# The order of a two-block network's steps on one Trainium2 core: found by a dry run, or written out as a table

## The chip, the core and the metric

The kernel runs on one core of a Trainium2 chip. The metric is the device time of one execution in microseconds (us); less is better. The core has five engines, each with its own queue of instructions that it takes in order: TensorE (PE, the matrix multiplications), VectorE (DVE), ScalarE (ACT), GpSimd (POOL), and SyncE (SP), which here only starts transfers from HBM. An instruction that waits for another engine holds up all that stands behind it on its own engine.

## The reference

256 tokens of width 1024 pass through two blocks, in float32. Cut to what matters:

```
def first_block(x, mem, ...):                 # two layers
    for l in range(2):
        mix = hybrid_mixer(h, w_in[l], ...)   # RG-LRU branch and sliding-window attention
        h = layer_norm(a * h + mix, ...)                                  # norm 1
        h = layer_norm(a * h + cross_attention(h, mem, cq_w[l], ckv_w[l], co_w[l]), ...)   # norm 2
        h = layer_norm(a * h + swiglu(h, ffn_wi[l], ffn_wo[l]), ...)      # norm 3
def second_block(x, c, ctx, ...):             # one layer
    sh_a, sc_a, g_a, sh_f, sc_f, g_f = split(silu(c) @ w_ada + b_ada, 6)  # the same for c_ctx
    h, hc = rms(x) * (1 + sc_a) + sh_a, rms(ctx) * (1 + csc_a) + csh_a
    q, k, v, u, vs = project(h, w_in_2); kc, vc = project_kv(hc, w_in_2)
    x = x + g_a * merge(neighborhood_attention(q, k, v, kc, vc, rpb), sgu(u, vs), w_out_2)
    hf = rms(x) * (1 + sc_f) + sh_f
    # 4 groups of 4 experts: one group for a token, two experts in it
    return x + g_f * hier_moe(hf, rg_w, re_w, w1, w3, w2)
```

The queries of the cross attention and all that follows depend on the norm before them; its keys and values (mem @ ckv_w) and the context's keys and values of the second block depend on no token, so they can be computed at almost any time before they are used.

## The kernel before

**Matrix products.** Float32 operands are split into a high and a low part, and a product takes three matmuls (mm3, L548 to L550: high by high, high by low, low by high). The 256 tokens stand as two tiles of 128, t0 and t1. A weight comes in units of 512 KB: SP loads one into a buffer (L343), ACT copies it to the high part (L433), DVE subtracts to get the low part (L434), and matmuls read both. There are 5 buffers for loaded units, besides others that are lent while they are free, and 6 for split ones. 564 units are split in one execution.

**Where tokens meet.** A layer norm (L716 to L735, one run for each tile of tokens) takes sums on DVE, squares on ACT (L720), a power on POOL (L731, L1485 and L1447 are such powers elsewhere), and writes its two halves on DVE (L735, twice for a tile). Then PE transposes the tile (L693, eight transposes), and ACT and DVE split what it wrote (L654, L655); only then can PE multiply that tile by the next weight. Head norms of keys and queries (L1480 to L1487) have the same form. Neighborhood attention (L1572 to L1595) and the gating and routing of tokens to experts (L1772 to L1849, then the gathering matmuls L1934) are further such chains.

**Order.** Each part of the network is a Python generator, a stream, that issues a few instructions and yields; `Streams.run` takes some streams (and filler streams, such as the keys and values named above) and picks whose next step is issued. In a first, dry pass over the whole network the picks come from a cost model, `Clock`, that holds a time for each engine; they are kept as a script, and the second pass, which issues the instructions, replays it. The dry pass also decides when weights are split ahead of their use (`step`, `extra`) beside the fixed rule of `prepare` (up to 4 units ahead), and after which weights a piece of the vector w_ada (L1412, L1414, "the trickle") is added up on DVE. The loads follow the order in which weights are used. `keep` and `drop` limit how many split units are held over several steps; the two filler lists of a layer's last two stages start only when the residual sums before a norm are done (`(1, 1) in seen`, `(1, 1) in over`).

```
        self.nc.scalar.activation(hi, raw, AF.Copy)                 # L433
        self.nc.vector.tensor_tensor(lo, raw, f(hi), op=OP.subtract)  # L434
```

Of the kernel before, what the change touches and what calls it, by code (L numbers as in the profile page):

```python
# [9 lines left out]
F = mybir.dt.float32  # L10
R = mybir.dt.float32r
# [20 lines left out]
def f(ap):  # L32

    return ap.bitcast(F)


class Clock:
# [155 lines left out]
class Streams:  # L193
# [76 lines left out]
class Net:  # L270
# [3 lines left out]
    def __init__(self, ctx, tc, io, out):  # L274
        self.tc, self.nc, self.io, self.out = tc, tc.nc, io, out
        pool = lambda name, bufs, **k: ctx.enter_context(tc.tile_pool(name=name, bufs=bufs, **k))
        self.const = pool("const", 1)
        self.wraw = pool("wraw", self.RAW)
        self.whi = pool("whi", self.HI)
        self.wlo = pool("wlo", self.HI)  # L280
        self.acts = pool("acts", self.ACTS)
        self.work = pool("work", 1)
        self.tiny = pool("tiny", 2)
        self.psum = pool("psum", 8, space=PS)
        dram = pool("dram", 1, space=bass.MemoryType.DRAM)
# [7 lines left out]
        self.cz = None  # L293
        self.time = Streams(each=self.step)

    def record(self, body, lend=True):

        kept = dict(vars(self))
        clock = Clock(self.io["x"].tensor, lambda: self.tick)
        self.nc = self.tc = clock  # L300
        for n in ("const", "wraw", "whi", "wlo", "acts", "work", "tiny"):
            setattr(self, n, Shelf(clock))
        self.psum = Shelf(clock, True)
        self.dry, self.time, self.plan, self.held = True, Streams(clock, each=self.step), list(self.plan), []
# [6 lines left out]
        self.plan, self.time, self.peak = plan, Streams(script=script, each=self.step), peak  # L311
        self.takes, self.extra, self.beats = takes, extra, beats

    def lasting(self, *tiles):
# [122 lines left out]
    def step(self):  # L437

        self.tick += 1
        if self.dry:  # L440
            t = self.nc.t
            if len(self.split_units) + len(self.held) < self.HI - 1 and max(t["vector"], t["scalar"]) + 1.0 < self.nc.now:
# [5 lines left out]
        if self.tick in self.extra:  # L448
            while len(self.ready) < len(self.loaded) and self.plan[len(self.ready)][2]:
                self._prep()  # L450
            if len(self.ready) < len(self.loaded) and len(self.splits) < self.HI:
                self._prep()
                self.preload()

    def preload(self):
        while len(self.loaded) < len(self.plan) and self.lender():
            self._load()

    def keep(self, n):

        while self.room < n:
            yield lambda: self.room >= n
        self.room -= n

    def drop(self, i):

        self.held.remove(i)
        self.room += 1

    def weight(self, src, cols=512, raw=False, kept=None):  # L470
# [4 lines left out]
            self.takes[i] = self.tick  # L475
        if self.dry:
            self.plan.append((src, cols, raw))
        self._free(i)
        self.prepare(i)
        w = self.ready[i]  # L480
# [15 lines left out]

    def prepare(self, i, taken=False):

        ahead = self.plan + [(None, 512, False)] * self.PREP_AHEAD if self.dry else self.plan
        end = min(len(ahead), i + 1 + self.PREP_AHEAD)  # L500
        while len(set([j for j in range(i, end) if not ahead[j][2]] + self.held)) > self.HI:
# [820 lines left out]
    def layer(self, l, h, hT, mem, fill, ready=None, after=None):  # L1322
# [28 lines left out]
        def memory():  # L1351
# [11 lines left out]
        run([self.cross_q_out(t, st) for t in range(2)] + [self.cross_heads(l, 0, st), self.cross_heads(l, 1, st)]  # L1363
            + self.norms(l, 1, old["hn"], res, new, self.transposes, lambda: ("os", 1) in st)
            + fill[1]() + [self.cross_q(l, old["hT"], st, old)]
            + [self.residual(lambda: st["cross"], self.io["co_w"][l], res, lambda q: ("os", q) in st)], fill[2](lambda: (1, 1) in seen))
# [4 lines left out]


        run(self.norms(l, 2, old["hn"], res, new, after or self.spilled, lambda: old.get(0) and old.get(1))
            + [self.first_hidden(t, first) for t in range(2)] + [self.ffn(l, old["hT"], res, old, first)], fill[3](lambda: (1, 1) in over))
        return (new["hn"] if after else self.spill), new["hT"], lambda t, q: t in new


# [856 lines left out]
def tile_net(ctx: ExitStack, tc: tile.TileContext, io, out, layers=L):  # L2234
# [126 lines left out]
```

## Time and profile before

| | |
|---|---|
| time, median of 3 runs | 1570.49 us (1568.84 to 1574.12) |
| time of the profiled execution | 1565.67 us |
| its span (first to last instruction) | 1563.9 us |
| mean granted clock of TensorE | 0.986 of full speed |
| PE busy | 1511.8 us (97%) |
| DVE busy | 1182.4 us (76%) |
| ACT busy | 904.3 us (58%) |
| POOL busy | 42.2 us (3%) |

The median is 4.8 us above the profiled execution. Busy times are sums over the span; matmuls overlap one another, and each end is modelled, so the 97% includes time in which PE ran at half its clock, and the latency of matmuls that stood alone. What PE did not do is 52 us, some of it at the two ends.

### The profile page before, as it was taken

To read this page: it belongs to the slowest core of one execution; us is meant where nothing else is said; L and a number is where in the kernel's file an instruction comes from. 1 tells how busy PE (TensorE), PEld (TensorE's weight loads), DVE (VectorE), ACT (ScalarE), POOL (GpSimd) and SP (SyncE) were. 2 spreads that over 40 slices of the span, in tenths; PEclk is the share of its full clock that TensorE was granted. 3 is DMA by queue.
4 is the path that set the end of the run, shared out by engine and by line. 5 is a ranking of instruction groups with operands and counts; after the bars stand their busy time and mean duration, and the time that the engine had idled before them with its cause. 6 is when DMAs were issued, how large, how long until landed. Compare 5 with 4: busy or idle time off the path is not lost. (4 is left out here: it accounts for less than half of the span.)

```text
span 1563.9 us, 24949 instructions
## 1 busy us (share of the span) xinstructions
PE 1511.8 (97%) x9594; PEld 1350.9 (86%) x9594; DVE 1182.4 (76%) x1713; ACT 904.3 (58%) x1348; POOL 42.2 (3%) x48
## 2 busy tenths in 40 slices
PE   8999999999999999999999899999899999999997
PEld 7999998987999989989988699998787778888886
DVE  6967876557887677869866677766676578999996
ACT  6687544444434455885556443444556468787773
POOL 0000000000000010000000100000120000000000
PEclk9999999999999999999999999999999989999999
DMA  9545676567677544347485577774554348999991
GB/s 340 165 149 180 224 258 218 178 202 235 218 262 234 202 162 135 109 164 254 153 305 179 184 236 240 239 242 149 182 189 135 123 146 311 394 376 391 377 330 43
DMA packets 194653, 344.57 MB, mean 220 GB/s; under 512 B 12384, under 2 KB 79840, under 8 KB 193632
## 3 DMA queue, kind: packets, MB, share of 16 engines
q1 hardware_dynamic: 193472, 339.76, 63.6%
q0 software_dynamic: 1056, 3.15, 0.6%
q8 instruction: 77, 1.26, 0.3%
q14 instruction: 48, 0.39, 0.1%
HBM read 339.71 MB, written 3.15 MB: 219 GB/s over the span
## 5 line engine op out<-in xcount | busy, mean ns | idle before, releaser
L548 PE MATMUL bank<-act,hi 128*128 128x256 f32 x1664 | 475.8, 286 | 0.0
L550 PE MATMUL bank<-act,lo 128*128 128x256 f32 x1664 | 470.8, 283 | 0.0
L549 PE MATMUL bank<-act,hi 128*128 128x256 f32 x1664 | 470.7, 283 | 0.0
L434 DVE TENSOR_TENSOR lo<-raw,hi 128x1024 fp32r<-128x1024 f32 x225 | 272.2, 1222 | 92.4 <-ACT hi L433 88.9
L548 PEld LDWEIGHTS bank<-act,hi 128*128 128x128 f32 x1664 | 319.0, 192 | 6.1 <-issue 4.5
L549 PEld LDWEIGHTS bank<-act,hi 128*128 128x128 f32 x1664 | 319.1, 192 | 1.2
L550 PEld LDWEIGHTS bank<-act,lo 128*128 128x128 f32 x1664 | 318.9, 192 | 0.0
L434 DVE TENSOR_TENSOR lo<-act,hi 128x1024 fp32r<-128x1024 f32 x229 | 273.4, 1221 | 57.2 <-ACT hi L433 56.1
L548 PE MATMUL bank<-hi,act 128*128 128x512 f32 (+1 forms) x784 | 304.8, 389 | 10.8 <-ACT hi L433 6.5
L550 PE MATMUL bank<-hi,act 128*128 128x512 f32 (+1 forms) x784 | 299.1, 381 | 0.0
L549 PE MATMUL bank<-lo,act 128*128 128x512 f32 (+1 forms) x784 | 298.4, 381 | 0.5 <-DVE lo L434 0.5
L433 ACT ACTIVATE hi<-raw 128x1024 fp32r<-128x1024 f32 x225 | 235.1, 1055 | 76.5 <-PE bank L549 44.5
L433 ACT ACTIVATE hi<-act 128x1024 fp32r<-128x1024 f32 x229 | 235.5, 1053 | 71.6 <-PE bank L549 34.4
L548 PEld LDWEIGHTS bank<-hi,act 128*128 128x128 f32 x784 | 149.9, 191 | 40.3 <-ACT act L654 7.2
L550 PEld LDWEIGHTS bank<-hi,act 128*128 128x128 f32 x784 | 149.2, 190 | 31.9 <-DVE act L655 4.1
L549 PEld LDWEIGHTS bank<-lo,act 128*128 128x128 f32 x784 | 149.7, 191 | 26.2 <-DVE lo L434 1.0
L434 DVE TENSOR_TENSOR lo<-k,hi 128x1024 fp32r<-128x1024 f32 x110 | 131.7, 1221 | 30.0 <-ACT hi L433 24.7
L433 ACT ACTIVATE hi<-k 128x1024 fp32r<-128x1024 f32 x110 | 114.7, 1057 | 47.2 <-PE bank L549 21.2
L548 PE MATMUL bank<-hi,k 128*128 128x512 f32 (+1 forms) x320 | 121.6, 380 | 0.0
L549 PE MATMUL bank<-lo,k 128*128 128x512 f32 (+1 forms) x320 | 121.5, 380 | 0.0
L550 PE MATMUL bank<-hi,k 128*128 128x512 f32 (+1 forms) x320 | 121.1, 378 | 0.0
L548 PEld LDWEIGHTS bank<-hi,k 128*128 128x128 f32 x320 | 60.2, 188 | 11.7 <-issue 0.8
(281 smaller groups left out, 1500.5 us busy)
## 6 DMA issues: line engine op xcount, KB each, us to landing
act<-in_w_dram SPq DMA_DIRECT2D x97, 512.0 KB, 6.8
raw<-in_w_dram SPq DMA_DIRECT2D x60, 512.0 KB, 6.5
raw<-in_w_in_dram SPq DMA_DIRECT2D x54, 512.0 KB, 4.0
act<-in_w_in_dram SPq DMA_DIRECT2D x42, 512.0 KB, 6.7
act<-in_ffn_wi_dram SPq DMA_DIRECT2D x80, 256.0 KB, 5.5
k<-in_w_dram SPq DMA_DIRECT2D x35, 512.0 KB, 6.8
act<-in_w_ada_dram SPq DMA_DIRECT2D x33, 512.0 KB, 6.3
raw<-in_ffn_wi_dram SPq DMA_DIRECT2D x64, 256.0 KB, 3.7
```

Of the source, the lines that this page charges most:

```text
L433: self.nc.scalar.activation(hi, raw, AF.Copy)
L434: self.nc.vector.tensor_tensor(lo, raw, f(hi), op=OP.subtract)
L548: mm(out, lhs[0], rhs[0], start=start, stop=False)
L549: mm(out, lhs[0], rhs[1], start=False, stop=False)
L550: mm(out, lhs[1], rhs[0], start=False, stop=stop)
```

## The change

The picks stand in the source as a table, ORDER: for each call of `Streams.run` a list of numbers, each the stream whose step comes next (a number is given to a stream when it is first handed to `run`), `5*2` for twice the same. Between them "s" stands for the split of one more unit (`split_next`) and "c" for one piece of the trickle (`add_up`). With a table, `keep`, `prepare`, the beats of the trickle, and the rule of `step` that splits ahead do nothing, and the filler lists may start at once. A stream's own conditions must hold where the table names it. The dry pass remains for the buffers. Only the rare overflow branch is still ordered by the cost model.

No arithmetic is added or left out. In all, PE has 9242 rows of instructions where it had 9240, DVE 1744 where it had 1747, ACT 1220 where it had 1222, POOL 55 and SP 846 as before. The order of the loads follows that of the uses.

```diff
@@ -32,6 +32,84 @@
+ORDER = """
+s 0 s 0*3 s*2 0 s*2
...
+s 26 21 20 21 20 s 26*3 21 32 26 20*3 32 26 21 26 32*2 s 32*5 21 32 30 21*4 31 26 s 21 32 s*2 32*4 s*2 c 32*5 s 32 31 s
...
+"""
+def order_of(table):
+    runs = []
+    for run in table.split(";"):
+        runs.append([])
+        for item in run.split():
+            what, _, times = item.partition("*")
+            runs[-1] += [int(what) if what.isdigit() else what] * int(times or 1)
+    return runs
@@ -199,7 +277,8 @@
-    def __init__(self, clock=None, script=None, each=None):
+    def __init__(self, clock=None, script=None, each=None, order=None, special=None):
+        self.order, self.special, self.live, self.waits = order, special, [], {}
@@ -211,6 +290,17 @@
+        if self.order is not None:
+            self.live += [g.stream if isinstance(g, Late) else g for g in list(main) + list(fill)]
+            for i in self.order.pop(0):
+                if i in self.special:
+                    self.special[i]()
+                    continue
+                assert self.waits.get(i, lambda: True)(), (i, len(self.order), self.live[i])
+                got = next(self.live[i], None)
+                self.waits[i] = got if callable(got) else lambda: True
+                self.each()
+            return
@@ -291,24 +381,28 @@
-    def record(self, body, lend=True):
+    def record(self, body, lend=True, order=None):
+        self.ordered = order is not None
+        special = {"s": self.split_next, "c": self.add_up}
...
@@ -437,6 +531,11 @@
+        if self.ordered:
+            if not self.dry:
+                self._free(self.at)
+                self.preload()
+            return
@@ -452,18 +551,34 @@
+    def split_next(self):
+        if self.dry:
+            return
+        while len(self.ready) < len(self.loaded) and self.plan[len(self.ready)][2]:
+            self._prep()
+        if len(self.ready) < len(self.loaded):
+            self._prep()
+            self.preload()
+    def add_up(self):
+        next(self.trickle, None)
...
@@ -475,6 +590,22 @@
+        if self.ordered:
+            if self.dry:
...
+            self._free(i)
+            while len(self.ready) <= i:
+                if len(self.loaded) <= len(self.ready):
+                    self._load()
+                self._prep()
+            w, self.ready[i] = self.ready[i], None
...
@@ -1371,7 +1504,7 @@
-            ... + [self.ffn(l, old["hT"], res, old, first)], fill[3](lambda: (1, 1) in over))
+            ... + [self.ffn(l, old["hT"], res, old, first)], fill[3](lambda: self.ordered or (1, 1) in over))
@@ -2275,7 +2408,7 @@
-    net.record(body)
+    net.record(body, order=order_of(ORDER))
```

Three places follow. Line numbers differ between the two files: L716 to L735 of before are L849 to L868 in the changed kernel, L655 is L788, L434 is L528, L731 is L864, L1485 is L1618. Numbers behind names count buffers.

On DVE in layer 0, after norm 2 and as the feed-forward stage begins, the norm of tile t1 ends with these rows before the change (k4_3780 and small_3786 belong to that norm; act_3713 is its result, which PE transposes):

```order
L727 SCALAR_TENSOR_TENSOR small_3785<-small_3785,eps_131 128x1
L728 SCALAR_TENSOR_TENSOR small_3786<-small_3783,small_3785 128x1
L434 TENSOR_TENSOR lo_3888<-act_3485,hi_3887 128x1024
L730 TENSOR_SCALAR small_3786<-small_3783,small_3786 128x1
L732 SCALAR_TENSOR_TENSOR k4_3780<-k4_3780,small_3784,act_3625 128x512
L434 TENSOR_TENSOR lo_3907<-raw_3493,hi_3906 128x1024
L1311 SCALAR_TENSOR_TENSOR k2_3925<-k2_3925,bank_3885 128x256
L1312 TENSOR_TENSOR k2_3925<-k2_3925,bank_3885 128x256
L735 SCALAR_TENSOR_TENSOR act_3713<-k4_3780,small_3786,act_3625 128x512 x2
L655 TENSOR_TENSOR act_3715<-bank_3933,act_3714 128x4x128
L655 TENSOR_TENSOR act_3715<-bank_3940,act_3714 128x4x128
```

And these with the change (k4_3761, small_3767, result act_3741):

```order
L857 TENSOR_SCALAR small_3765<-small_3763 128x1
L858 TENSOR_SCALAR small_3766<-small_3763 128x1
L859 SCALAR_TENSOR_TENSOR k4_3761<-k4_3761,small_3765,act_3739 128x512
L860 SCALAR_TENSOR_TENSOR small_3766<-small_3766,eps_131 128x1
L861 SCALAR_TENSOR_TENSOR small_3767<-small_3764,small_3766 128x1
L528 TENSOR_TENSOR lo_3882<-raw_3491,hi_3881 128x1024
L863 TENSOR_SCALAR small_3767<-small_3764,small_3767 128x1
L865 SCALAR_TENSOR_TENSOR k4_3761<-k4_3761,small_3765,act_3739 128x512
L868 SCALAR_TENSOR_TENSOR act_3741<-k4_3761,small_3767,act_3739 128x512 x2
L788 TENSOR_TENSOR act_3743<-bank_3916,act_3742 128x4x128
L788 TENSOR_TENSOR act_3743<-bank_3923,act_3742 128x4x128
```

The split lo_3907 and the two additions of a gate (L1311, L1312) no longer stand between the norm's last scaling and its result; one split stays ahead of it.

On DVE after norm 3 of layer 0, as layer 1 begins, the end of the norm of tile t1 before the change (result act_5822):

```order
L730 TENSOR_SCALAR small_5946<-small_5943,small_5946 128x1
L732 SCALAR_TENSOR_TENSOR k4_5940<-k4_5940,small_5944,act_3947 128x512
L735 SCALAR_TENSOR_TENSOR act_5822<-k4_5940,small_5946,act_3947 128x512
L434 TENSOR_TENSOR lo_6042<-act_5647,hi_6041 128x1024
L434 TENSOR_TENSOR lo_6052<-act_5700,hi_6051 128x1024
L925 TENSOR_TENSOR k2_6074<-act_5876,rope_121 128x128
L926 TENSOR_TENSOR k2_6074<-act_5876,rope_121 128x8x8
L927 TENSOR_TENSOR k2_6074<-act_5876,rope_121 128x8x8
L928 TENSOR_TENSOR act_5876<-k2_6074 128x8x16
L735 SCALAR_TENSOR_TENSOR act_5822<-k4_5940,small_5946,act_3947 128x512
L655 TENSOR_TENSOR act_5824<-bank_6080,act_5823 128x4x128
L655 TENSOR_TENSOR act_5824<-bank_6087,act_5823 128x4x128
```

With the change (result act_5834):

```order
L861 SCALAR_TENSOR_TENSOR small_5922<-small_5919,small_5921 128x1
L863 TENSOR_SCALAR small_5922<-small_5919,small_5922 128x1
L865 SCALAR_TENSOR_TENSOR k4_5916<-k4_5916,small_5920,act_5262 128x512
L868 SCALAR_TENSOR_TENSOR act_5834<-k4_5916,small_5922,act_5262 128x512 x2
L528 TENSOR_TENSOR lo_6052<-act_5652,hi_6051 128x1024
L788 TENSOR_TENSOR act_5836<-bank_6055,act_5835 128x4x128
L788 TENSOR_TENSOR act_5836<-bank_6062,act_5835 128x4x128
L528 TENSOR_TENSOR lo_6071<-act_5652,hi_6070 128x1024
L528 TENSOR_TENSOR lo_6076<-k4_5717,hi_6075 128x1024
```

Two splits and a rotary embedding (L925 to L928) stood between the two halves of the result, and nothing does now. On PE, the two tiles' transposes had 24 matmuls of 128x512 between them at this place; now 18 of these and 54 of 128x256 stand there, the latter from the cross attention's keys and values of layer 1.

On POOL after norm 2 of layer 1, before the change (small_9344 and small_9391 are the norm's powers for t0 and t1, small_9477 is that of a context key's head norm, an 8-column power):

```order
L731 TENSOR_TENSOR small_9344<-small_9344,half_129 128x1
L1485 TENSOR_TENSOR small_9477<-small_9476,half_129 128x8
L731 TENSOR_TENSOR small_9391<-small_9391,half_129 128x1
L1424 DMA rspill_84<-k2_10962 16x1x32
L731 TENSOR_TENSOR small_11421<-small_11421,half_129 128x1
```

With the change (the norm's powers are small_9342 and small_9396):

```order
L864 TENSOR_TENSOR small_9342<-small_9342,half_129 128x1
L864 TENSOR_TENSOR small_9396<-small_9396,half_129 128x1
L1618 TENSOR_TENSOR small_9721<-small_9720,half_129 128x8
L1557 DMA rspill_84<-k2_11156 16x1x32
L864 TENSOR_TENSOR small_11419<-small_11419,half_129 128x1
```

The head norm's power came between the two of the norm; it now follows them, and the steps of that key that read it (L1480 to L1487 on ACT and DVE, four transposes on PE) have moved behind the feed-forward stage's first matmuls.

## Rows read from the trace of the kernel before

**Rows 1.** The page: busy time (part 1), and GB/s in 40 slices (part 2).
```profile
PE 1511.8 (97%) x9594; PEld 1350.9 (86%) x9594; DVE 1182.4 (76%) x1713; ACT 904.3 (58%) x1348; POOL 42.2 (3%) x48
...
GB/s 340 165 149 180 224 258 218 178 202 235 218 262 234 202 162 135 109 164 254 153 305 179 184 236 240 239 242 149 182 189 135 123 146 311 394 376 391 377 330 43
```

**Rows 2.** Waits of PE, largest first: total us, times, longest.
```profile
PE bank L693 <- DVE act L735: 4.8, 2, 2.8
...
PE bank L693 <- DVE k L1487: 4.2, 2, 2.8
```

**Rows 3.** Windows: length, busy time of each engine, PEclk, DMA share, GB/s.
```profile
318.00:342.00 24.00, 22.57 (x104) 18.11 (x103) 11.19 (x14) 10.68 (x17) 0.00 (x0) 1.00 0.52 167
355.00:373.00 18.00, 14.92 (x63) 11.01 (x62) 11.89 (x21) 8.69 (x14) 1.58 (x2) 0.91 0.72 241
553.00:583.00 30.00, 26.95 (x166) 23.86 (x165) 21.56 (x38) 14.54 (x23) 4.23 (x6) 0.94 0.51 175
818.00:882.00 64.00, 60.67 (x330) 50.69 (x331) 37.88 (x62) 37.30 (x70) 3.03 (x3) 1.00 0.50 164
882.00:902.00 20.00, 14.88 (x90) 13.42 (x90) 17.62 (x40) 9.33 (x16) 3.99 (x3) 0.93 0.73 236
1110.00:1135.00 25.00, 20.46 (x92) 16.50 (x92) 15.23 (x29) 15.12 (x27) 5.07 (x5) 0.86 0.70 240
1170.00:1235.00 65.00, 58.45 (x324) 44.90 (x323) 37.40 (x97) 34.38 (x71) 3.21 (x5) 0.92 0.40 128
1235.00:1265.00 30.00, 25.48 (x141) 21.68 (x140) 21.66 (x52) 12.71 (x23) 2.77 (x5) 0.87 0.42 144
1300.00:1553.00 253.00, 252.66 (x1209) 211.38 (x1207) 230.50 (x233) 192.21 (x221) 0.00 (x0) 1.00 0.88 326
```

**Rows 4.** Timeline of DVE and PE, 355 to 373: start, us, instruction, idle before.
```profile
362.01 1.22 DVE L434 TENSOR_TENSOR lo<-raw,hi 128x1024 fp32r<-128x1024 f32 x1
...
364.16 1.41 DVE L735 SCALAR_TENSOR_TENSOR act<-k,small,act 128x512 f32<-128x512 f32 x2
...
364.96 1.32 PE L693 MATMUL bank<-ident,act 128*128 128x128 f32 x8 [2.05 <-DVE act L735]
```

**Rows 5.** Timeline of PE and DVE, 553 to 576.
```profile
553.27 0.28 PE L549 MATMUL bank<-act,hi 128*128 128x256 f32 x1
553.39 0.28 PE L550 MATMUL bank<-act,lo 128*128 128x256 f32 x1
...
571.38 0.39 PE L549 MATMUL bank<-lo,act 128*128 128x512 f32 x1
571.61 0.39 PE L550 MATMUL bank<-hi,act 128*128 128x512 f32 x1
...
571.23 2.35 DVE L434 TENSOR_TENSOR lo<-act,hi 128x1024 fp32r<-128x1024 f32 x2
...
574.30 0.74 DVE L735 SCALAR_TENSOR_TENSOR act<-k,small,act 128x512 f32<-128x512 f32 x1
...
575.19 1.09 PE L693 MATMUL bank<-ident,act 128*128 128x128 f32 x4 [2.75 <-DVE act L735]
```

**Rows 6.** Timeline of POOL and PE, 893 to 902.
```profile
895.50 2.08 POOL L1485 TENSOR_TENSOR small<-small,half 128x8 f32<-128x8 f32 x1 [1.11 <-DVE small L1484]
897.71 0.98 POOL L731 TENSOR_TENSOR small<-small,half 128x1 f32<-128x1 f32 x1
...
899.61 1.12 PE L693 MATMUL bank<-ident,k 128*128 128x128 f32 x4 [2.76 <-DVE k L1487]
```

**Rows 7.** Timeline of PE, 1253 to 1264.
```profile
1262.98 1.37 PE L1934 MATMUL bank<-act 128*128 128x256 f32 x3 [1.07 <-DVE act L1849]
```

**Rows 8.** Transfers of the experts' weights: times, KB each, median us to landing.
```profile
act<-in_w_dram SPq DMA_DIRECT2D x97, 512.0 KB, 6.8
raw<-in_w_dram SPq DMA_DIRECT2D x60, 512.0 KB, 6.5
...
k<-in_w_dram SPq DMA_DIRECT2D x35, 512.0 KB, 6.8
```

More of the change, by code (lines that the diff above doesn't have):

```diff
@@ new lines @@
+11 s 5*3 s*2 5 11*2 s*2 11*11 5 11 5*2 s 11 5 s 11 s 6 11 12*3 s 12*2 s 12*7 s 12*8 6 12*5 14 6 12*4 s*2 12 s 12*3 13*5
+7 13 6 13*5 6 s 13*11 c s 7 8 9 s 8*3 9 s*2 9 s*2 6 8*2 6
+;
+22 25 14*3 25 15 25 8*2 14*7 s*2 14 25 14 9*2 14 8 14*2 s*2 9*2 25*2 8 25 14*4 21 c 24*2 s 9 24 9 8*2 s*2 17 8 14*2 9
+14*3 9 s*2 20 14 22*2 14 22 9*2 22*2 25*2 14 22*7 s*3 c 22*4 15 22*2 14*2 24 22 s 26 22*2 24 22 14*2 s*5 14 22 14*2 16
+14 16 15 s 14*2 23 14 16 14 17*4 22 14 22 s 25 22*2 18 22 17 s 22*4 s 14*2 s 22*2 17 s 18 17 23 24 18 17 23 18*3 s*2 23
@@ new lines @@
+s 32*3 s 32*6 s c 32*2 s*3 32*2 s 32*9 s 27 28 s 28*5 34 s 28*2 s 29 33 28
+;
+34*2 33 28 34*2 s 29 33 s 33 s 28*2 33 28 34 33 35*7 33*3 29*8 35 34*3 s 29*2 34 s 29 s 33*2 35*4 s 35*5 34 35
+;
+s*3 40*7 s 40*11 s 40 42 37 45 s*2 38 c*2 45*8 40*7 39 40*3 36 40*7 c 40 s 45*4 s 45 s*2 37 40*3 s 36 s 37 45 37 36*2 45
+40 45*2 38 45 38*2 s 40 39 s 39 38 45 40 45 38 47 45 43 40 39 s 40*2 46 39*2 40*2 38 39 45*2 40 38 s*2 38 41 s 38 45*2
+40 45*6 s 45 38 45 s 45*3 40 45*7 39 38 s 45*2 40 s 38 49 45*3 39*2 s 45*2 38 45 s 40 39 45 39*2 38*2 48 45 s 45 39 s 38
@@ L293, in __init__ @@
         self.cz = None
+        self.ordered = False
         self.time = Streams(each=self.step)
-    def record(self, body, lend=True):
+    def record(self, body, lend=True, order=None):
+        self.ordered = order is not None
+        special = {"s": self.split_next, "c": self.add_up}
+        given = lambda: dict(order=[list(x) for x in order], special=special) if self.ordered else {}
         kept = dict(vars(self))
@@ L303, in record @@
         self.psum = Shelf(clock, True)
-        self.dry, self.time, self.plan, self.held = True, Streams(clock, each=self.step), list(self.plan), []
+        self.dry, self.time, self.plan, self.held = True, Streams(clock, each=self.step, **given()), list(self.plan), []
         self.ready, self.split_units, self.raw_units, self.ring = [None] * self.at, [], [], []
@@ L310, in record @@
         vars(self).update(kept)
-        self.plan, self.time, self.peak = plan, Streams(script=script, each=self.step), peak
+        self.plan, self.time, self.peak = plan, Streams(script=script, each=self.step, **given()), peak
         self.takes, self.extra, self.beats = takes, extra, beats
@@ L459, in keep @@
     def keep(self, n):
-        while self.room < n:
+        while not self.ordered and self.room < n:
             yield lambda: self.room >= n
@@ L465, in drop @@
     def drop(self, i):
+        if self.ordered and self.dry:
+            return
         self.held.remove(i)
@@ L477, in weight @@
             self.plan.append((src, cols, raw))
+        if self.ordered:
+            if self.dry:
+                if kept is not None:
+                    kept.append(i)
+                w = [self.wraw.tile([128, 1024], F if raw else R).rearrange("p (k c) -> p k c", c=cols) for _ in range(2)]
+                return (w[0], None) if raw else tuple(w)
+            self._free(i)
[4 more added lines that the diff above has]
+            w, self.ready[i] = self.ready[i], None
+            if kept is not None:
+                self.held.append(i)
+                kept.append(i)
+            return w
         self._free(i)
@@ L497, in prepare @@
     def prepare(self, i, taken=False):
+        if self.ordered:
+            return
         ahead = self.plan + [(None, 512, False)] * self.PREP_AHEAD if self.dry else self.plan
@@ L1365, in layer @@
             + fill[1]() + [self.cross_q(l, old["hT"], st, old)]
-            + [self.residual(lambda: st["cross"], self.io["co_w"][l], res, lambda q: ("os", q) in st)], fill[2](lambda: (1, 1) in seen))
+            + [self.residual(lambda: st["cross"], self.io["co_w"][l], res, lambda q: ("os", q) in st)], fill[2](lambda: self.ordered or (1, 1) in seen))
         old, res, new = new, self.marks(), self.marks()
@@ L1373, in layer @@
         run(self.norms(l, 2, old["hn"], res, new, after or self.spilled, lambda: old.get(0) and old.get(1))
-            + [self.first_hidden(t, first) for t in range(2)] + [self.ffn(l, old["hT"], res, old, first)], fill[3](lambda: (1, 1) in over))
+            + [self.first_hidden(t, first) for t in range(2)] + [self.ffn(l, old["hT"], res, old, first)], fill[3](lambda: self.ordered or (1, 1) in over))
         return (new["hn"] if after else self.spill), new["hT"], lambda t, q: t in new
```

46 lines of the change are left out of this document (added).

## The prediction

> **What bounds the kernel now.** The page comes first: PE is busy for 1511.8 us of 1563.9 [rows 1], so nearly all of the time is matmul work that the change doesn't touch, and an order can win at most what PE loses. The idle part is 52 us. Part of it lies at the two ends, where the order moves nothing: the first matmul waits for the first weight, and additions and the store follow the last one. The list of PE's waits shows no wait for a transfer behind the start, but waits for DVE, ACT and POOL in front of transposes: for the last write of a norm (L735) and for a head norm (L1487) [rows 2]. The windows then show where they lie [rows 3]. In a window I count as lost the time in which PE isn't busy, and the share of the clock that wasn't granted times the window: 355 to 373 loses 18 - 14.92 = 3.1 us and 0.09 x 18 = 1.6 us, so 4.7. In the same way 318 to 342 loses 1.4, 553 to 583 4.9, 818 to 882 3.3, 882 to 902 6.5, 1110 to 1135 8.0: **28.8 us in six places** around the norms. 1170 to 1235 loses 11.8 and 1235 to 1265 8.4: **20.2 us** in neighborhood attention, gating and routing. The clock column says that a stall is paid more than once: where PE stands, the granted clock of the stretch is 0.86 to 0.94, a mixture of its two levels, 1.2 and 2.4 GHz, and it is 1.00 in the windows with less idle time. The experts' stage, 1300 to 1553, has PE busy 252.66 us of 253: nothing to win, and DVE is busy 230.5 us of it.
>
> **What the change does, part by part.** The instructions are the same but for a few rows, so their cost is nothing; what counts is what stands ahead of what. Three places first.
>
> Layer 0, after norm 2. PE waits 2.05 us for the result of tile t1's norm, whose two halves begin on DVE at 364.16; a split of 1.22 us that began at 362.01 and a gate's two additions stand just ahead of them [rows 4]. The new order has neither there: 364.16 - 362.01 = 2.15 us off this chain. It also puts 12 key and value matmuls of 128x256 between the two tiles' transposes, beside the 24 feed-forward ones; a matmul of 128x256 follows its forerunner by 0.12 us, one of 128x512 by 0.23 us [rows 5], so 1.4 us more cover. Together 3.5 us against a wait of 2.05. Against that, tile t0's transposes, from which DVE goes on, stand earlier in the new order by 18 such matmuls, and the cover ends within about half a microsecond of the chain. I leave 0.4 of the 4.7 us.
>
> Layer 0, after norm 3. PE waits 2.75 us; the second half of t1's result, at 574.30, stands behind two splits and a rotary embedding that begin at 571.23, so 3.07 us are of others' making [rows 5]. With the change nothing stands between the halves, and PE has 18 x 0.23 + 54 x 0.12 = 10.6 us of work between the two tiles' transposes where it had 24 x 0.23 = 5.5. I leave 0.3 of 4.9. If the cover were gone, the 3.07 us would still be off.
>
> Layer 1, after norm 2. POOL's power for the context key takes 2.08 us, and that of t1's norm starts behind it at 897.71; PE waits 2.76 us for the key and then for the norm [rows 6]. In the new order both norm powers come first and the key's steps stand in the feed-forward stage, where 128x256 matmuls cover them. PE's matmuls of the context's projection stand between the four transposes. I leave 0.5 of 6.5.
>
> The other three have the same form, with less to see: at 318 to 342 one matmul still stands behind a split, and I count no gain (1.3 stays); at 818 to 882 key and value matmuls are spread between the steps of the cross attention, and 1.3 of 3.3 stays; at 1110 to 1135 the head norm and both tiles' scalings are laid between four units of the context's projection, and 1.4 of 8.0 stays, where tile t1's result is split behind two copies on ACT. What stays is an estimate: I added up the durations of before along the new sequence of DVE, ACT and POOL, and compared with PE's work in between. Sum: 28.8 - 0.4 - 0.3 - 0.5 - 1.3 - 1.3 - 1.4 = 23.6 us. The bounds are 23.6 and about 8, the latter if only what is taken out of the chains counts (2.15 + 3.07 + 2.76) and no cover holds.
>
> Attention, gating and routing. Here the chain itself is long: a softmax goes DVE, ACT, PE, ACT, PE for each pair of heads, and the gathering matmuls at 1262.98 wait 1.07 us at the end of a run of small DVE steps [rows 7], while little other matmul work is left. The new order puts output units between pairs of heads, but the last tile's routing still stands bare. Bounds: nothing and 12 us of 20.2; I take 5, near the lower one, since the chain's own instructions stay.
>
> The experts' stage. Splits are placed by the table, the third product's matmuls stand somewhat later. PE doesn't idle there, so the gain is nothing; a loss is possible. The splits' cover is DVE's 22 idle us. Between a split's place and its first use PE has under 1.5 us of work for 14 units in the new order, and for 25 in the old. The last unit's load stands 6.5 us of matmuls ahead of its split, where it stood 13.8, and loads take 6.5 to 6.8 us [rows 8]: some tenths at the end. For this, and for waits that adding up by hand doesn't see, I take off 4 us; the bounds are 0 and 12.
>
> Sum: 23.6 + 5 - 4 = 24.6 us, from 1565.67 of the profiled execution to 1541.1. The median lies 4.8 us above that execution, so **1546 us**.
>
> **Weighed against a rule.** The slices from about 1290 to 1486 us move 376 to 394 GB/s [rows 1]. The 192 experts' units of 512 KB [rows 8] are 100.7 MB; at 6 matmuls of 0.23 us a unit PE needs about 1.38 us each, 265 us in all, and at 385 GB/s the transfers need 261, so neither holds up the other, as PE's 252.66 of 253 us says. The Trainium skill, "DMA: Bandwidth & Descriptors", section Specifications, gives a limit of some 358 GB/s for a core from HBM. By it the same bytes would take an estimated 281 us, the experts' stage would be paced by transfers, and what is won after their first load would be lost again: 19.6 us in place of 24.6. The trace disagrees with it here: 376 to 394.
>
> **Rivals.**
> *The stalls move on.* The margins at 355 and 882 are about half a microsecond. If 355, 882 and 1110 kept their losses (4.3 + 6.0 + 6.6 = 16.9) and attention won nothing, 23.6 - 16.9 - 4 = 2.7 us would be left: 1568, no change. Against it: at each of them the rows show others' work inside the chain, which is gone.
> *Half of it.* Chains are shorter, but cover fails in places: 8 to 18 us, about 1557.
> *Slower: late splits of the experts.* ACT and DVE take splits in the table's order, and a split that waits for its load holds up all behind it, where the old rule kept up to four units ahead. If in each of 16 experts PE waited for one pair of copy and subtraction, some 2.3 us, that would be 37 us: 24.6 + 4 - 37, so 8 us slower, 1579. It decides from 28.6 / 16 = 1.8 us an expert. For it: DVE's 230.5 us of 253 [rows 3]. Against it: fewer units with a short distance than before.
> *More.* All covers hold and attention gives 12 us: 36 us, 1535.
> *Transfers pace the experts*, as a mechanism of this kernel: if the loads, at nearly PE's own rate, could not follow an earlier start, what is won from 1170 on would be lost: 19.6 us, 1551. For it, 385 against 380 GB/s (512 KB in 1.38 us); against it, PE's lack of idle time there. The page's rule stands above.
> *The change does nothing*, because the table repeats the old picks: excluded by the rows of the order.
>
> **How the numbers follow.** Forecast (18 to 32 us won) 0.48; half of it 0.18; more 0.12; transfers 0.06; the stalls move on 0.08; late splits 0.08. A measurement of this kernel can tell 0.3%, or 4.7 us, from no change. So faster 0.48 + 0.18 + 0.12 + 0.06 = 0.84, same 0.08, slower 0.08. The range reaches to 1533, just past the case of more, and to 1563 (8 us), and leaves out slower, same and the extremes of more.
>
> **What would show it.** The transposes at some 360, 570, 890 and 1110 us should no longer wait above 0.5 us, and L735 and L1487 should leave the head of PE's waits; the clock of these stretches should be 1.00. The experts' stage should last 253 us as before. PE's busy time should fall by some us too, as stretches at half the clock go. Wrong would be: new waits of PE for L433 or L434 behind the start; a norm's transposes that wait again, a few rows later; or an experts' stage longer than 253 us.

## The result, and the profile after

The changed kernel takes **1508.32 us** (median of 4 runs, 1507.89 to 1509.57), beside 1569.66 us for the kernel before (4 runs): a ratio of 0.9605, 95% interval 0.9585 to 0.9626. Forecast was 1546, with 1533 as the low end: the sign was right, and the gain more than twice what was foreseen. The profiled execution took 1508.56 us, with a span of 1506.8 us, 57.1 less than before.

The page of the changed kernel, parts 1 and 2 (beside [rows 1]):

```profile
PE 1485.1 (99%) x9594; PEld 1340.4 (89%) x9594; DVE 1179.6 (78%) x1713; ACT 899.7 (60%) x1348; POOL 45.1 (3%) x48
GB/s 346 177 137 181 215 283 178 203 231 276 222 220 261 203 196 134 125 154 206 240 209 212 221 258 232 212 280 196 168 232 153 168 196 338 371 387 369 378 321 58
```

The counts behind the x are those of before: no work was added or left out.

PE's waits in the changed kernel, largest first (beside [rows 2]):

```profile
PE bank L681 <- ACT hi L527: 6.3, 1, 6.3
PE bank L1979 <- DVE oh L1961: 1.8, 2, 1.4
PE bank L2067 <- DVE act L1982: 1.1, 1, 1.1
```

The first is the wait for the first weight, the next two are the routing, all but 0.4 us of them that of the last tile. The norms' last write (L868, once L735) and the head norms (L1620, once L1487) are gone from the list.

Where the time came from can be read by matching stretches of equal matmul work. I added up, in both traces, each matmul's usual distance from its forerunner (the median of its shape), and looked where the two sums agree. The nine windows of [rows 3] become these (length, busy time of each engine, PEclk, DMA share, GB/s):

```profile
315.00:336.80 21.80, 21.80 (x104) 18.33 (x104) 11.70 (x16) 10.33 (x18) 0.00 (x0) 1.00 0.79 271
349.80:361.90 12.10, 12.10 (x62) 10.08 (x61) 10.03 (x16) 6.68 (x8) 0.99 (x1) 1.00 0.86 295
541.70:566.40 24.70, 24.70 (x167) 22.78 (x166) 19.52 (x33) 11.61 (x18) 3.79 (x6) 1.00 0.56 193
799.40:857.30 57.90, 57.90 (x327) 51.07 (x326) 37.02 (x59) 36.57 (x68) 1.07 (x2) 1.00 0.67 210
857.30:870.60 13.30, 13.21 (x86) 11.89 (x85) 11.26 (x25) 8.29 (x15) 0.99 (x1) 1.00 0.85 289
1078.60:1095.80 17.20, 16.43 (x90) 13.77 (x89) 11.15 (x22) 13.40 (x25) 2.16 (x3) 1.00 0.61 214
1130.70:1183.60 52.90, 52.72 (x329) 41.84 (x328) 38.62 (x103) 37.01 (x76) 4.47 (x6) 1.00 0.45 149
1183.60:1209.80 26.20, 23.05 (x138) 20.30 (x137) 19.73 (x44) 11.57 (x22) 2.09 (x3) 0.91 0.46 161
1243.90:1495.90 252.00, 252.00 (x1208) 211.55 (x1207) 230.33 (x235) 194.22 (x221) 0.54 (x1) 1.00 0.88 326
```

The reader is to compare lengths: 24 us became 21.8, 18 became 12.1, 30 became 24.7, 64 became 57.9, 20 became 13.3, 25 became 17.2. The six places around the norms gave 2.2 + 5.9 + 5.3 + 6.1 + 6.7 + 7.8 = **34.0 us**. The two windows of attention, gating and routing gave 12.1 + 3.8 = **15.9**, the experts' stage **1.0**. The remaining 6.2 of 57.1 lie in short waits outside these windows, 2.0 to 2.3 of them in each layer's sliding-window attention.

### The profile page after: what moved, and what is told of

Same layout as the page of the kernel before. It is cut to its first block, busy times and chain, and to the rows that moved or that the text cites. A ratio compares the mean times of both kernels' runs of the same rounds, so it can differ in the third digit from the quotient of the medians.

```text
span 1506.8 us, 24927 instructions
## 1 busy us (share of the span) xinstructions
PE 1485.1 (99%) x9594; PEld 1340.4 (89%) x9594; DVE 1179.6 (78%) x1713; ACT 899.7 (60%) x1348; POOL 45.1 (3%) x48
## 5 line engine op out<-in xcount | busy, mean ns | idle before, releaser
L528 DVE TENSOR_TENSOR lo<-act,hi 128x1024 fp32r<-128x1024 f32 x250 | 297.3, 1220 | 53.9 <-ACT hi L527 51.9
L681 PE MATMUL bank<-hi,act 128*128 128x512 f32 (+1 forms) x784 | 301.6, 385 | 7.1 <-ACT hi L527 6.3
L683 PE MATMUL bank<-hi,act 128*128 128x512 f32 (+1 forms) x784 | 296.2, 378 | 0.0
L527 ACT ACTIVATE hi<-act 128x1024 fp32r<-128x1024 f32 x250 | 257.2, 1054 | 57.0 <-PE bank L682 30.3
L528 DVE TENSOR_TENSOR lo<-raw,hi 128x1024 fp32r<-128x1024 f32 x214 | 256.5, 1219 | 28.7 <-ACT hi L527 27.4
L527 ACT ACTIVATE hi<-raw 128x1024 fp32r<-128x1024 f32 x214 | 221.6, 1054 | 57.9 <-PE bank L682 25.1
L681 PEld LDWEIGHTS bank<-hi,act 128*128 128x128 f32 x784 | 148.1, 189 | 34.7 <-ACT hi L527 6.3
L683 PEld LDWEIGHTS bank<-hi,act 128*128 128x128 f32 x784 | 147.8, 189 | 28.3 <-DVE act L788 0.7
L528 DVE TENSOR_TENSOR lo<-k,hi 128x1024 fp32r<-128x1024 f32 x100 | 120.3, 1219 | 16.8 <-ACT hi L527 16.2
L527 ACT ACTIVATE hi<-k 128x1024 fp32r<-128x1024 f32 x100 | 104.0, 1054 | 22.3 <-PE bank L682 13.5
```

The lines of the kernel that those rows point to most:

```text
L681: mm(out, lhs[0], rhs[0], start=start, stop=False)
L683: mm(out, lhs[1], rhs[0], start=False, stop=stop)
```

## Experiments

Old picks were put into parts of the table, to see which part earns what. The old order is known as a list: which stream is picked, and where splits and pieces of the trickle fall. Steps already done by then are dropped from it.

**First eight tables: mixed, and flawed.** They took the two loads of some weight units of the second block for one, so that the new parts lacked two splits and the old ones four; a unit that isn't split by the time it is used is split on demand, and what is in the table behind it comes late. The first four also put each old split behind its step. Old picks stand in the whole table (e1), in the last call of `Streams.run`, which begins ahead of attention and holds the place at 1110 to 1135 too (e2), from the first unit of w1 on (e3), and from attention to routing (e4); the diff shows a line of the table in e2.

```diff
-97 98 66 67*2 104 66 97 66*2 98*4 97*2 67 98 67*6 96 98*5 74 75 99 98*2 101 74 98*3 100 77 110 98 100 s*2 98 75*2 99*3
...
+110 111 112 113 114 115 116 117 118 119 120 121 66 67 97 66 67 97 66 67*2 97 67 66 98*2 s 74 98*2 s 67 98*4 67 98 75
```

> The machinery of the new kernel with the old picks written into its table, in every stage. If the order alone makes the difference (theory): the time of before, 1570, within 0.3%. If reading the order from a table changes something by itself (rival: the splits' places, the additions between steps): some us off 1570, toward the 1508 of the changed kernel.

> New order in both layers, old order from neighborhood attention to the end. Theory A, stages add up (matched by equal PE work, the two traces part by 39 us up to the start of attention, by 17 in attention, gating and routing, by 0.5 in the experts' stage): 39 us faster than before, 1530. Theory B, the prediction's sizes (norms 24, attention 5): 1546 at best. Theory C, the layers' gain is partly bought by handing matmul work on to attention: under 30 us here, 1540 or more, with a longer attention than before's.

> New order up to the first unit of the experts' weights, old order behind it. Theory A: within 0.3% of the changed kernel, 1508 to 1512, PE without idle time in the experts' stage in either order. Rival, the late splits' price that the prediction took off (4 us) is real and was won back by the new order elsewhere in that stage: 4 us faster than the changed kernel, 1504; or the new placing of the splits itself earned something: 1512 to 1520.

> New order in both layers and in the experts' stage, old order in attention, gating and routing. Theory A: 17 us slower than the changed kernel, 1525, with PE's waits in attention as in before (20 us lost). Theory B (attention is worth 5): 1513. Theory C (attention's gain rests on work that the layers leave for it): more than 17 us slower, 1530 or more.

Measured: 1587.28, 1553.34, 1523.25 and 1539.43 us (before 1567.13; ratios 1.0123 with 1.0093 to 1.0153, 0.9914 with 0.9882 to 0.9947, 0.9716 with 0.9689 to 0.9742, 0.9819 with 0.9789 to 0.9848). The old picks came out 20 us slower than before, so none of the four says what a stage is worth: they mix the stage with late splits. No whole table of old picks was run with all splits, but e1's trace answers the rival that the table earns something by itself. Matched by work, its PE stands within 0.1 us of the kernel before at 318 and at 600 us, and its waits for a norm's last write are those of before (third line; [rows 2] has 4.8 in two). Of the 22.7 us by which its span is longer, 2.3 come ahead of 1135 us and the rest behind, where PE waits for splits (its line numbers are 11 above those of the changed kernel; the first line holds 6.3 us for the first weight):

```profile
PE bank L692 <- ACT hi L538: 8.6, 4, 6.3
PE bank L693 <- DVE lo L539: 7.9, 16, 0.9
PE bank L837 <- DVE act L879: 4.8, 2, 2.7
```

The next four put old splits inside their steps, and still lacked the same ones. f2 and f3 have the parts of e2 and e3; f4 has old picks from the last projection unit to the first output unit, f5 from there to the first unit of w1.

```diff
-        special = {"s": self.split_next, "c": self.add_up}
+        self.inside = []
+        special = {"s": self.split_next, "c": self.add_up, "a": lambda: self.inside.append(self.split_next), ...
...
             w, self.ready[i] = self.ready[i], None
+            while self.inside:
+                self.inside.pop(0)()
```

> New order in both layers, the old picks from neighborhood attention to the end, with each split standing inside the step in which the dry run put it, unlike the runs before. Theory A, stages add up: 39 us faster than before (1528 to 1531), attention, gating and routing lose 20 us as in before, the experts' stage lasts 253 us. Theory C, attention's gain rests on what the new layers leave for it: 1540 or more. If the splits' places explain the 23 us between the first two runs, this one is some 20 us faster than the run with new layers and late splits (1553).

> New order up to the first unit of the experts' weights, behind it the old picks with each split inside its step. Theory A: the changed kernel's time within 0.3% (1508 to 1512): nothing to win or to lose in the experts' stage by itself. The prediction's allowance (new placing costs 4 us there): 1504. Rival (the table's placing of splits earned something): 1515 or more.

> The changed kernel, with the old picks only between the last projection unit and the first output unit: the softmax chains of neighborhood attention and the gating beside them. Theory A, the order of the small steps among each other is what keeps PE fed there: 8 us slower than the changed kernel (1516), with waits of PE for ACT's exponentials and for their transposes. Rival, the gain comes from the output units that are kept for later, and the chains' own order is worth little: under 3 us slower (1511).

> The changed kernel, with the old picks only from the first output unit to the first unit of the experts' weights. Theory A: 9 us slower than the changed kernel (1517), with waits of PE for the norms of the tiles and for routing. Rival (the last tile's routing stands bare in either order, so nothing is to be won): under 2 us slower.

Measured: 1553.12, 1524.24, 1533.70 and 1531.40 us (before 1567.86; ratios 0.9900 with 0.9877 to 0.9923, 0.9718 with 0.9697 to 0.9738, 0.9771 with 0.9743 to 0.9799, 0.9759 with 0.9736 to 0.9783). The place of a split inside its step was not the cause: the first two stayed at 1553 and 1524. The trace of f3_experts_old shows the cause, more than 100 us ahead of the old picks (timeline of PE and ACT; its line numbers are 7 to 13 above those of the changed kernel):

```profile
1091.79 0.79 PE L694 MATMUL bank<-hi,act 128*128 128x512 f32 x1 [4.69 <-ACT hi L534]
...
1088.11 0.63 ACT L800 ACTIVATE act<-k 128x512 fp32r<-128x512 f32 x1 [2.64 <-DVE k L1616]
1088.64 1.49 ACT L1614 ACTIVATE k<-bank,mod 128x128 f32<-128x128 f32 x4
1090.16 0.63 ACT L800 ACTIVATE act<-k 128x512 fp32r<-128x512 f32 x1
1090.69 1.99 ACT L534 ACTIVATE hi<-raw 128x1024 fp32r<-128x1024 f32 x2
```

The window behind it, in the same run (columns as above):

```profile
1088.30:1098.30 10.00, 6.05 (x13) 4.42 (x14) 6.08 (x7) 6.24 (x10) 0.00 (x0) 0.50 0.41 119
```

The copy of the unit (L534) stands on ACT behind the splits of both tiles' activations (L800, once L654) and a scaling, in place of ahead of them; PE waits 4.69 us, and the stretch is at half the clock. With the splits restored, and else the same:

> New order in both layers, the old picks from neighborhood attention to the end, now with every split of the old order (the eight runs before lacked two or four splits of the first projection units, so that the later splits stood late). Theory A, stages add up: 39 us faster than before (1528 to 1531), attention, gating and routing lose 20 us as in before, the experts' stage lasts 253 us. Theory C, attention's gain rests on what the new layers leave for it: 1540 or more.

> New order up to the first unit of the experts' weights, the old picks behind it, no split missing. Theory A: the changed kernel's time within 0.3% (1508 to 1512). The prediction's allowance (the new placing costs 4 us there): 1504. Rival (the table's placing of the experts' splits earned something): 1515 or more.

> The changed kernel, with the old picks only between the last projection unit and the first output unit, no split missing. Theory A, the order of the small steps of the softmax chains and the gating keeps PE fed there: 6 to 8 us slower than the changed kernel (1515), lost inside that stretch, behind waits of PE for ACT and for transposes; the earlier version with missing splits lost 6.6 us there. Rival, the gain comes from the output units kept for later: under 3 us slower (1511).

> The changed kernel, with the old picks only from the first output unit to the first unit of the experts' weights, no split missing. Theory A: 9 us slower than the changed kernel (1517), with waits of PE in front of the tiles' transposes and of routing. Rival (the last tile's routing stands bare in either order, so nothing is to be won): under 2 us slower.

| run | us (4 runs) | ratio to before (1568.41), 95% | against 1508.32 | same table with splits missing |
|---|---|---|---|---|
| g2: layers new, then old | 1529.38 | 0.9753, 0.9735 to 0.9772 | +21.1 | 1553.12 |
| g3: old from w1 on | 1510.00 | 0.9629, 0.9611 to 0.9648 | +1.7 | 1524.24 |
| g4: old in the softmax stretch | 1515.20 | 0.9660, 0.9641 to 0.9679 | +6.9 | 1533.70 |
| g5: old from output units to w1 | 1521.36 | 0.9698, 0.9673 to 0.9722 | +13.0 | 1531.40 |

The 1508.32 us were measured apart from these runs. By the ratios, the interval of g3 overlaps that of the changed kernel (0.9585 to 0.9626), and those of the other three don't. So the experts' picks are worth nothing that can be told: 1.7 us is within 0.3%. Two to four missing splits of some 560 cost 10 to 24 us.

Stages add up to within some us: g3, g4 and g5 lose 21.6 us together, g2 21.1, though g2's old part holds the place at 1110 to 1135 too. That g2's 39.0 us are just theory A's 39 is in part luck, since theory A counted the gain at that place, and in g2 PE waits 2.3 us there again. g2's traced execution took 1535.5 us (the other three 1529.2 to 1529.4); its span is 30.2 us shorter than that of before. Theory C falls: in attention PE's waits are those of before (2.7 us in three waits for L1736, which is L1590 of before, in both), so nothing there shows work that the new layers took away; that this trace reads 0.50 in attention from 1156 to 1163 once more than before changes no wait.

That the order inside attention and routing is worth much is shown by g4 and g5. In g4 PE has two waits in attention that the changed kernel hasn't (timeline of PE, DVE, POOL and ACT):

```profile
1148.38 1.10 PE L1728 MATMUL bank<-act,k 128*128 128x64 f32 x8 [0.96 <-ACT k L1723]
...
1159.69 0.66 PE L826 MATMUL bank<-ident,act 128*128 128x128 f32 x4 [2.34 <-ACT act L1818]
...
1155.30 1.13 DVE L1809 SCALAR_TENSOR_TENSOR k<-bank,c2t,k 128x128 f32<-128x128 f32 x4 [0.58 <-PE bank L1805]
...
1157.77 1.10 POOL L1580 TENSOR_TENSOR small<-small,half 128x1 f32<-128x1 f32 x2 [4.24 <-DVE small L1579]
...
1158.92 0.71 ACT L1818 ACTIVATE act<-k,small 128x512 f32<-128x512 f32 x1
```

Two windows of g4, ahead of the longer wait and behind it:

```profile
1150.00:1160.00 10.00, 7.66 (x59) 6.02 (x56) 7.33 (x27) 6.16 (x15) 2.28 (x4) 1.00 0.40 129
1160.80:1167.60 6.80, 6.80 (x28) 4.97 (x28) 3.55 (x8) 2.84 (x7) 0.00 (x0) 0.50 0.36 98
```

PE waits for the transposes' input, the gate's scaling (L1818). That needs a power on POOL, which starts at 1157.77: the squares ahead of it on ACT wait for the gate's second product (L1809), and this comes on DVE only at 1155.30, behind a softmax's steps. A copy and an exponential of the softmax stand ahead of the scaling on ACT too, from 1157.78; they hold it some 0.6 us more (an estimate: half of the two powers' 1.10 us puts the first at 1158.3). In the changed kernel the products of both tiles stand together, the powers start at 1155.53, both scalings follow, and 16 matmuls of two pairs of heads stand between them and the transposes (timeline of DVE, POOL, ACT and PE):

```profile
1152.29 2.15 DVE L1809 SCALAR_TENSOR_TENSOR k<-bank,c2t,k 128x128 f32<-128x128 f32 x8
...
1155.53 1.10 POOL L1580 TENSOR_TENSOR small<-small,half 128x1 f32<-128x1 f32 x2 [3.62 <-DVE small L1579]
...
1156.48 1.32 ACT L1818 ACTIVATE act<-k,small 128x512 f32<-128x512 f32 x2
...
1156.88 2.00 PE L1728 MATMUL bank<-act,k 128*128 128x64 f32 x16
1158.72 1.04 PE L826 MATMUL bank<-ident,act 128*128 128x128 f32 x8
```

No matmul was brought in from elsewhere for this: the chain's own steps were put in another order. The two waits, 3.3 us, and half of the 6.8 us at 0.50 are 6.7 us, which is what g4 loses by work where the changed kernel runs from 1130.7 to 1183.6.

g5 shows the same form (timeline of PE, ACT and DVE; its line numbers are 7 above those of the changed kernel):

```profile
1173.54 1.10 PE L1735 MATMUL bank<-act,k 128*128 128x64 f32 x8 [0.66 <-ACT k L1730]
1176.72 1.97 PE L1735 MATMUL bank<-act,k 128*128 128x64 f32 x8 [2.08 <-ACT k L1730]
...
1175.40 0.69 ACT L1725 ACTIVATE k<-bank,small 128x512 f32<-128x512 f32 x1 [1.92 <-DVE small L1720]
...
1176.08 1.07 ACT L1730 ACTIVATE k<-bank 128x512 f32<-128x512 f32 x2
...
1173.03 1.23 DVE L529 TENSOR_TENSOR lo<-act,hi 128x1024 fp32r<-128x1024 f32 x1 [0.26 <-ACT hi L528]
1174.18 0.42 DVE L1716 TENSOR_REDUCE small<-bank 128x1 f32<-128x256 f32 x1
```

The copies that PE waits for (L1730) stand on ACT behind an exponential that waits 1.92 us for DVE, where its maximum (L1716) stands behind a weight's split. In the changed kernel, half a microsecond ahead of g5 here, the same maximum stands at 1167.13, with the other three:

```profile
1167.13 0.41 DVE L1709 TENSOR_REDUCE small<-bank 128x1 f32<-128x256 f32 x1
```

The window of g5 behind the wait of 2.08 us:

```profile
1176.60:1186.50 9.90, 9.78 (x36) 7.66 (x37) 3.32 (x9) 3.65 (x8) 0.00 (x0) 0.50 0.33 125
```

The waits and half of this window are 7.7 us, of 8.1 that g5 loses by work in the same stretch; 3.9 more come in the routing behind it.

**Chain or cover at a norm.** After norm 3 of layer 0 ([rows 5]) the change did two things: others' work left the chain, and matmuls were put between the two tiles' transposes. p1 takes back part of the second, p2 puts others' work into the chain again.

```diff
 # p1_cover_moved: 36 matmuls of streams 33 and 34 behind tile t1's steps (stream 29)
-... 35*7 33*3 29*8 35 34*3 s 29*2 34 s 29 s 33*2 35*4 s 35*5 34 35
+... 35*7 29*8 35 s 29*2 s 29 s 33*3 34*4 33*2 35*4 s 35*5 34 35
 # p2_chain_mixed: two splits and stream 35's rotary embedding between the halves of t1's result
+... 35*9 33*3 29*7 s*2 35 29 34*3 29*2 34 s 29 33*2 35*2 s 35*5 34 35
```

> The changed kernel, with 36 of the 54 matmuls of keys and values that stand between the two tiles' transposes after norm 3 of layer 0 moved behind tile t1's; DVE's order is untouched. In the changed kernel t1's result is written at 555.3 us and its transposes begin at 558.1; 36 x 0.12 us taken away, PE comes there at 553.8. Theory A, the cover counts: PE waits 1.6 us for the norm's last write, and if the clock falls behind that wait as it did behind 2.3 us in the run before (6.8 us at half clock), 5 us are lost in all, else 1.6. Theory B, the others' work that left the chain is what counts: no wait of PE there and no time lost.

> The changed kernel, with two splits and the rotary embedding put back between the two halves of t1's result after norm 3 of layer 0, as in the kernel before, and with the six matmuls that the embedding needs ahead of the keys and values; all matmuls that stand between the tiles' transposes stay there. Theory A, the cover counts: the result comes some 3 us later, at about 558.3, PE reaches the transposes at about 559.5, nothing is lost. Theory B, the chain's length counts: up to 3.1 us slower, with a wait of PE for the norm's last write.

Measured: 1510.30 us for p1 (ratio to before, at 1566.77: 0.9636, 0.9617 to 0.9655) and 1513.21 for p2 (0.9655, 0.9636 to 0.9674), 2.0 and 4.9 above the changed kernel; p1's interval overlaps that of the changed kernel, p2's doesn't. The timeline of PE in p1, with a wait of 0.79 us where theory A had 1.6, and no fall of the clock:

```profile
555.10 1.38 PE L826 MATMUL bank<-ident,act 128*128 128x128 f32 x8 [0.79 <-DVE act L868]
```

In p2, with all that cover and six matmuls more, it waits 3.41 us (timeline of PE, DVE and ACT):

```profile
564.59 0.63 PE L826 MATMUL bank<-ident,act 128*128 128x128 f32 x4 [3.41 <-DVE act L868]
...
556.20 0.75 DVE L868 SCALAR_TENSOR_TENSOR act<-k,small,act 128x512 f32<-128x512 f32 x1 [0.46 <-POOL small L864]
559.60 1.23 DVE L528 TENSOR_TENSOR lo<-act,hi 128x1024 fp32r<-128x1024 f32 x1 [2.65 <-ACT hi L527]
561.76 1.22 DVE L528 TENSOR_TENSOR lo<-k,hi 128x1024 fp32r<-128x1024 f32 x1 [0.94 <-ACT hi L527]
...
563.70 0.74 DVE L868 SCALAR_TENSOR_TENSOR act<-k,small,act 128x512 f32<-128x512 f32 x1
...
558.51 1.06 ACT L527 ACTIVATE hi<-act 128x1024 fp32r<-128x1024 f32 x1 [4.04 <-PE bank L682]
```

The window around it in p2:

```profile
545.00:578.00 33.00, 29.59 (x206) 27.45 (x205) 23.79 (x40) 16.06 (x22) 3.24 (x5) 1.00 0.51 173
```

The second half came not 3 us after the first, as theory A had it and as it did before, but 563.70 - 556.95 = 6.75: DVE's subtraction waits for ACT's copy, the copy waited 4.04 us and was let go by a matmul of PE, and DVE, which takes its queue in order, keeps the norm's half waiting all that time. Matmuls that stand between the transposes don't cover this, since the split waits for some of them. What the releaser frees was not tried apart; the six split buffers of the kernel are the likely thing. Before the change DVE's two subtractions at this place ran without a wait (2.35 us, [rows 5]), so p2 isn't the old chain again. Matched by work, p1 loses 1.3 us at this place and p2 3.6, of 5.3 that the change won there. So 4.3 us of cover could go for 1.3, and splits in the middle of a norm cost more than they last; whether theory A's cover would have hidden the old chain's 3 us, and what cover and chain are worth apart, neither run shows.

## Why the prediction was wrong in size

**What bounds the kernel** was right: PE, with the gain in what it loses, and no wait for a transfer behind the start. In the windows, [rows 3] and above, the experts' stage was the flat one.

**The three places looked at closely** moved as said: no wait of L826 is left at any of them, the clock reads 1.00, and the granted clock rose from 0.986 to 0.996 over the span. PE's busy time fell too, by 26.7 us, and no wait for L527 or L528 above 0.5 us came up behind the start. The statement that the 3.07 us of others' work would be off even without the cover is not borne out. From the start of tile t0's transposes to the end of t1's second half (L735, L868) 574.30 + 0.74 - 564.67 = 10.4 us passed before; now it is 553.92 + 1.42 - 546.64 = 8.7, and 8.7 in p1 too, so 1.7 us less (PE before, then PE and DVE of the changed kernel):

```profile
564.67 1.04 PE L693 MATMUL bank<-ident,act 128*128 128x128 f32 x8
...
546.64 1.04 PE L826 MATMUL bank<-ident,act 128*128 128x128 f32 x8
...
553.92 1.42 DVE L868 SCALAR_TENSOR_TENSOR act<-k,small,act 128x512 f32<-128x512 f32 x2 [0.46 <-POOL small L864]
```

Two splits (from 546.09, 2.35 us) now hold DVE while t0 is transposed, and both sums of t1's norm come behind them, where before one sum stood ahead of t0's transposes. So part of the cover was needed: with 6.3 us of it in place of 10.6, PE waits 0.79 us in p1.

**The step that failed most is the term for attention, gating and routing.** It took 5 us of 20.2, "near the lower one, since the chain's own instructions stay". They stayed, and 15.9 us came, 3.9 above the upper bound of 12. g4 and g5 show why: what PE waited for was not the chain's own length but the order of two tiles' and several streams' steps on DVE and ACT and in PE's own queue. The reasoning that little other matmul work is left looked for cover from outside; the chains cover each other. The routing of the last tile does stand bare, as said: 2.9 us of waits (L1979, L2067) remain in the routing, all but 0.4 of them the last tile's, and the clock falls there too (0.91 in the window from 1183.6).

**The six places: 23.6 taken, 34.0 measured.** The upper bound of 23.6 was wrong too. I took the idle time and the clock not granted, 28.8 us, for all that PE loses. A wait costs more than it shows (PE in the kernel before, with its old line numbers):

```profile
872.75 0.50 PE L548 MATMUL bank<-hi,act 128*128 128x512 f32 x1 [0.69 <-ACT act L654]
873.09 0.40 PE L549 MATMUL bank<-lo,act 128*128 128x512 f32 x1
873.48 0.50 PE L550 MATMUL bank<-hi,act 128*128 128x512 f32 x1
873.81 0.39 PE L548 MATMUL bank<-hi,act 128*128 128x512 f32 x1
```

Behind a wait of 0.69 us the next three distances are 0.34, 0.39 and 0.33 us, where 0.23 is usual: 0.37 us more, counted as busy. Over the span the idle time fell by 52.1 - 21.7 = 30.4 us. By the mean clock, 0.014 x 1563.9 = 21.9 us were not granted before and 0.004 x 1506.8 = 6.0 after, so 15.9. Together 46.3 of 57.1. The other 11 are found at the waits too, if each matmul's distance beyond the usual one of its shape is added up where the clock reads 1.00: the last matmul ahead of each wait, whose end no next one hides, makes 7.2 us before and 2.0 now, and the four behind each wait 7.4 and 1.6, so 11.0 less (an estimate: ends of matmuls are modelled). At 318 to 342, where I counted 0.1 us of gain, 2.2 came, and at 818 to 882 6.1 where I counted 2.0: their waits of 0.7 us were each small, and the new order has none of them.

**The allowance of 4 us** for the experts' stage was not needed: the stage gave 1.0, and g3 shows that old and new picks there are alike within what can be told.

**Outside all windows** 6.2 us came that the sum had not looked at. By parts the sum falls short by 34.0 - 23.6 = 10.4, 15.9 - 5 = 10.9, 1.0 + 4 = 5.0 and 6.2: 32.5 us, which is 57.1 - 24.6. The rest of the miss is mostly the 4.8 us that I added for the median: the profiled execution before was below its median, the one after was not.

**The rivals.** Stalls did not move on. Late splits did not happen, but their mechanism is real: the tables with two to four splits missing lost 10 to 24 us by it, and with the old picks it made the kernel 20 us slower than before (e1). Transfers do not pace the experts: the stage begins 56 us earlier, the slices from 1280 to 1431 us move 369 to 387 GB/s, and it lasts 252 us. (Before the change, 376 to 394 GB/s begin at 1329 us, not at about 1290 as I wrote; the slice from 1290 moved 311.) So the trace of after too disagrees with the limit of some 358 GB/s in the Trainium skill, "DMA: Bandwidth & Descriptors", section Specifications. "More" was the right rival, with too low a ceiling.

## What to carry to other kernels

To price a better order, match both traces by work done, or take as ceiling all that the bounding engine loses: idle time, the clock not granted, and the slower matmuls at each wait. A long dependent chain is no lower bound while two copies of it, one for each tile, can cover each other; look at what stands ahead of the awaited instruction on each engine, and at what the waiting engine has next in its queue. Never put a step that waits for a resource of the bounding engine, like the split of a weight in p2, into the chain that this engine waits for.

## What was not expected of the hardware

A wait is not always followed by a fall of the clock. In g4, after a stretch in which PE was busy 7.66 of 10 us, with 59 recorded matmuls, most of them of 64 or 128 columns, a wait of 2.34 us was followed by a window at 0.50, that is the lower level, 1.2 GHz. In p2 a longer one, 3.41 us, lay in a stretch that reads 1.00 throughout, with PE working through matmuls of 256 and 512 columns without a gap before and after it. In f3 a wait of 4.69 us was followed by 10 us at 0.50, in which PE was busy 6.05. In the kernel before, waits of 2.05 and 2.75 us at two norms, where PE also works on matmuls of 256 and 512 columns, were each followed by a stretch at 0.50 (windows behind 364.96 and around 575.19):

```profile
367.00:370.00 3.00, 3.00 (x8) 2.40 (x8) 0.64 (x1) 0.86 (x1) 0.00 (x0) 0.50 0.95 370
575.00:578.00 3.00, 2.81 (x9) 2.46 (x10) 1.34 (x3) 0.60 (x1) 0.58 (x1) 0.50 0.43 175
```

So the length of a wait alone doesn't give its price: 3.41 us cost no clock, 2.05 and 2.75 us some 3.4 us at half of it each, 2.34 us 6.8 (g4), 2.08 us 9.9 (g5). What decides is not shown by these runs. A price taken from one wait can be off by several us at another.
